# A two-layer SSD and HGRN2 trunk on one core: weight sums begun one iteration later, a spill cut into four, two gate operations given priority, and new amounts of filling work

## The chip, the cores and the metric

The kernel runs on one core of a Trainium2 chip. The core has a matrix engine (TensorE, PE in the profile), a vector engine (VectorE, DVE), a scalar engine that evaluates functions and copies (ScalarE, ACT), a general engine (GpSimd, POOL), and SyncE (SP), which here only issues transfers. Each engine takes its own instructions one after the other in a fixed order, and instructions on different engines wait for each other through semaphores. Transfers between the chip's memory (HBM) and the core's memory (SBUF) run in queues; the two that matter here are the one that SP issues (q1 in the profile) and the one that POOL issues (q0). The results of matmuls stand in PSUM, in banks of 128x512 numbers of 4 bytes.

The metric is the device time of one execution in microseconds (us), as the median of several executions. Less is better.

## The reference, cut to what matters

Two layers work on x of 512 tokens by 1024 features. Layer 0 mixes tokens with a Mamba-2 SSD (inner width 2048, 32 heads of 64, 4 groups, state 128), layer 1 with HGRN2 (8 heads of 128).

```python
for i in range(2):
    mix = ssd_mixer(x, ...) if i == 0 else hgrn2_mixer(x, ...)
    h = layer_norm(ALPHA * x + mix)
    h = layer_norm(ALPHA * h + square(relu(h @ w1)) @ w2)        # w1: 1024 x 4096
    x = h + sigmoid(h @ ple_w_gate[i]) * (p[i] @ ple_w_proj[i])  # p[i]: 512 x 256
# ssd_mixer:   z, xbc, dt = split(u @ w_in); xbc = silu(conv4(xbc)); scan over chunks of 128;
#              y = rms_norm((scan + d * xs) * silu(z)); y @ w_out
# hgrn2_mixer: q, fz, v, g = split(u @ w_in); k = (1 - lb) * sigmoid(-fz); scan over chunks;
#              rms_norm(o) * silu(g) @ w_out
```

All of it is in 32-bit floating point.

## The kernel before, in words

**Products.** The kernel gives TensorE operands of the type `fp32r`; it writes every operand as a high part and a low part and forms each product with three matmuls (`mm3`, lines 120 to 122: high by high, high by low, low by high). For weights, `unit` (line 103) loads 512 KB into a `raw` buffer through SP's queue; ACT casts it to `whi` (line 114), DVE subtracts for `wlo` (line 116), and PE takes them as they are done. The pools have 3 `raw` buffers, 6 of `whi` and 6 of `wlo`, 9 of a larger kind called `b8`, and 4 PSUM banks called `pj`. A unit is 1.05 us of ACT, 1.22 us of DVE and, in the SSD stage, 24 matmuls.

**Who sets the order.** The order of PE's instructions is the order of the code, by hand (`tc.manual_schedule`). Those of ACT, DVE, POOL and SP are put into an order at build time by a scheduler, which goes by readiness in its own model and by priorities: `high_priority(LEAD)` for weights (100), `high_priority(TURN)` for some steps of the gate (200); `behind(x)` keeps an instruction from being issued ahead of x. On the chip the order is then fixed: an instruction that waits holds all that stand behind it on its engine.

**SSD stage (0 to some 340 us).** After a start that makes the token operand out of four chunks of x and runs the first group of products (`py`, lines 170 to 174), a loop over k = 1 to 8 holds one product of 128 channels after the other: `x_part(2k)`, `x_part(2k+1)` (products whose convolution starts with ACT's line 810 and ends with line 816), `z_part(2k-2)`, `z_part(2k-1)` (silu in line 866, `sz`), `decays` (exponentials on ACT, lines 900 to 914, L907, L911 and L912 among them), `states`, `mixed`, and `finish` (which normalises; ACT's line 976 makes `ri`). The z parts stand so for k = 2 to 6; `z_part(12)` follows at k = 7, and `z_part(13)`, `z_part(14)` and, later, `z_part(15)` at k = 8. DVE's line 246 adds a piece of the output product from a `pj` bank into `acc`.

**Sums of weights.** HGRN's v and g products, and the MLPs', use a block product of 2 x 2 blocks with seven products in place of eight; its operands are sums of blocks of the weights and of the tokens. The sums of the weights for HGRN are made during the SSD stage, by `sums_early` (line 426): eight pieces, each a `b8` buffer, four loads of 256 KB on POOL's queue (line 433), two steps of two DVE operations (lines 436 to 441), and two steps of two ACT casts (line 448), two DVE subtractions (line 449) and four stores to `pre_h` (lines 450 and 451). So a piece is five steps, and all of them 40; the loop calls `next(sums)` at five places per k, from k = 1 on.

**Gate of layer 0 and start of HGRN (to some 790 us).** `mlp_and_gate` ends with the gate h @ gate, whose `finish(c, h, sg)` (line 662) multiplies a product by `sg` (line 669) and adds it to `acc` (line 670). Afterwards `turn` (line 620) transposes a chunk of `acc` on PE (line 624) into the operand of HGRN; ACT and DVE split it (lines 627 and 628), and `mix_part` (line 593) makes the sums of tokens. The last two turns stay in the list `late`.

**HGRN.** The scan's instructions on PE leave it idle unless other products stand between them. `background` (line 1198) is a generator of such products, one matmul triple at a time: the first eight triples of `gated(0)`, the late turns, a spill of all of `acc` (2 MB, line 1204, POOL's queue) to `xd`, since `blocks_late` (line 1147, copies in lines 1153 and 1154) takes the memory of `acc`, and then the entries of `JOBS`: `q0` to `q7` are `qf` (a head's q and f products; ACT copies the first into `qx`, line 1167, and makes f and k of the second, lines 1171 and 1174), `s` is `blocks_late`, `b0` and `b1` are `gated(0)` and `gated(1)` (the v and g products; each holds two `pj` banks, and line 1142 adds its last ones to v), `o` the first half of the output product. `restore` reads `xd` back. `fill(n)` takes n us of that work; `GAPS` has an n for each gap between the scan's stages, a row for each pair of heads. The first matmul on a tile v is in line 1409.

Of the kernel before, what the change touches and what calls it, by code (L numbers as in the profile page):

```python
# [29 lines left out]
TURN = 200  # L30
# [3 lines left out]

JOBS = "q0 q1 s q2 q3 b0 q4 q5 q6 q7 b1 o".split()
LEADIN = 6.0
GAPS = (6.0, 12.0, 9.0, 9.0), (11.0, 10.0, 10.0, 10.0), (10.5, 10.5, 10.5, 10.5), (10.5, 7.0, 4.0, 3.5), (3.0, 2.0, 2.5, 0.0)
CONSTS = dict(ident=P, triu=P, eps=1, convw=96, convb=24, dskip=16, snw=16, dtc=2, hlb=8, hnw=1)
# [3 lines left out]
def trunk(ctx: ExitStack, tc, a):  # L42
# [382 lines left out]
    def sums_early(w, dst):  # L425

        for u in range(2):
            for h in range(2):
                cs = slice(h * 512, (h + 1) * 512)
                t = mk(b8, [P, 4, T], "b8", F32R)  # L430
                w00, w01, w10, w11 = (f32(t)[:, i] for i in range(4))
                for x, src in zip((w00, w01, w10, w11), (w[0][0], w[0][1], w[1][0], w[1][1])):
# [82 lines left out]
    def mlp_and_gate(layer, h_s, last, turns=()):  # L515
# [79 lines left out]
        def mix_part(h, c, v):  # L595

            cs = slice(c % 2 * P, c % 2 * P + P)
            if not mix:
                mix["keep"] = mk(b8, [P, 2, 4, 256], "b8")
            k0, k1 = (mix["keep"][:, i, :, cs] for i in range(2))  # L600
            if c < 2:
                if h:
                    nc.vector.tensor_sub(k0, v, k0)
                else:
                    nc.scalar.copy(k0, v)
                return
            if c == 2:
                mix["s2" if h else "s3"] = mk(b8, [P, 2, 4, 256], "b8", F32R)
            if h:
                nc.vector.tensor_add(k1, v, k1)  # L610
                nc.vector.tensor_sub(k0, k1, k0)
                put("s2", cs, k0)
            else:
                nc.scalar.copy(k1, v)
                s3 = tmp("sg", [P, T]).rearrange("p (j t) -> p j t", j=4)
                nc.vector.tensor_sub(s3, k0, v)
                put("s3", cs, s3)
# [42 lines left out]
        def finish(c, h, sg):  # L660
# [5 lines left out]
            for i, part in enumerate(pp):  # L666
                cs = slice(i * n, (i + 1) * n)
                d = acc[:, c, h * 512 + i * n : h * 512 + (i + 1) * n]
                nc.vector.tensor_mul(sg[:, cs], part, sg[:, cs])
                (nc.vector if i == len(pp) - 1 else nc.gpsimd).tensor_add(d, sg[:, cs], d)  # L670
                if last:
# [324 lines left out]
    heads = [[[[whvg[8 * i + 4 * n + 2 * r + u] for u in range(2)] for n in range(2)] for r in range(2)] for i in range(2)]  # L996
    sums = (step for i in range(2) for step in sums_early(heads[i], a["pre_h"][i]))

    PIECES = {3: (0, 4), 4: (2, 2), 5: (0, 4), 6: (2, 2)}

    with tc.manual_schedule(engines={mybir.EngineType.PE}):
# [8 lines left out]
        for k in range(1, 9):  # L1010
# [11 lines left out]
            states(k - 1)  # L1022
            next(sums)
            decays(i - 1)
            some(mine)
            next(sums)
            if k < 8:
                load_decay(i)
                x_part(j)
                load_decay(j)  # L1030
            if k in (3, 5, 7):
                outs = pieces(k // 2 - 1, rms_group(k // 2 - 1, bank(psy, "py0")))
            some(theirs)
            next(sums)
            if k == 1:
# [10 lines left out]
            if k == 2:  # L1046
                nc.sync.dma_start(acc, a["x"])
                for c in range(NCH):
                    nc.vector.tensor_scalar(acc[:, c, :], acc[:, c, :], ALPHA, None, ALU.mult)
            next(sums)  # L1050
            done = [mixed(i - 2), (mixed(i - 1))] if k != 7 else [mixed(12)]
# [7 lines left out]
            for t, d in enumerate(done):  # L1059
                finish(i - 2 + t, *d)  # L1060
            next(sums)
        some(3)
# [135 lines left out]
    def background():  # L1198
# [3 lines left out]
        for f in late:  # L1202
            f()
        nc.gpsimd.dma_start(a["xd"], acc)
        for job in JOBS:
            i = int(job[1:] or 0)
            if job == "o":
                yield from out0()
            elif job == "s":
                blocks_late()  # L1210
            elif job[0] == "q":
# [389 lines left out]
```

## Time and profile before

| | us |
|---|---|
| median of 3 runs (1401.05 to 1402.51) | 1402.27 |
| the profiled execution, whole | 1401.34 |
| its span (first to last instruction) | 1399.6 |
| TensorE busy in it | 1387.8 (99%) |
| VectorE busy | 1104.3 (79%) |
| ScalarE busy | 820.5 (59%) |
| GpSimd busy | 62.6 (4%) |

The mean granted clock of TensorE is 0.999. Times inside the kernel are counted from the start of the span. A row of the timeline has the start, the duration, the engine, the line, the operation, its output and inputs (buffer numbers left out), and, in brackets, how long the engine stood idle ahead of it and what ended that. A row of the waits has the waiting engine's operation, what it waited for, the sum in us, how many times, and the largest. Matmuls are pipelined: each takes some 0.4 us, and the next one starts before it ends.

### The profile page before, as it was taken

How to read it: one execution, taken by the hardware profiler on the slowest of the kernel's cores; microseconds unless marked ns; L12 is line 12 of the kernel's file. 1: busy time of each engine (PE TensorE's matmuls, PEld its weight loads, DVE VectorE, ACT ScalarE, POOL GpSimd, SP SyncE). 2: the span in 40 equal slices, each digit the busy share in tenths (PEclk: the TensorE clock that was granted, in tenths of full speed). 3: DMA queues.
4: the chain of work that ended last, by engine and by line, in shares of the span. 5: the costliest groups of instructions: out<-in, count | busy, mean ns of one | idle time of the engine just before them, and what ended most of it. 6: DMA issues, size and time to landing. Idle time of an engine off the chain costs nothing.

```text
span 1399.6 us, 20799 instructions
## 1 busy us (share of the span) xinstructions
PE 1387.8 (99%) x7909; PEld 1159.1 (83%) x7909; DVE 1104.3 (79%) x1750; ACT 820.5 (59%) x1329; POOL 62.6 (4%) x122
## 2 busy tenths in 40 slices
PE   9999999999999999999999999999999999999998
PEld 7888888888888888888887788888898888888887
DVE  7898887788867879778888766768785887779886
ACT  6897777596455455546465355464455464555563
POOL 0121210211000000000000000000000000000000
PEclk9999999999999999999999999999999999999999
DMA  7566555554364665654384553464173656646364
GB/s 288 201 232 208 195 177 185 204 176 163 113 206 149 216 220 166 212 191 154 118 303 167 198 194 109 152 228 150 61 256 114 213 175 223 215 159 207 106 237 157
DMA packets 79252, 258.75 MB, mean 185 GB/s; under 512 B 9776, under 2 KB 10416, under 8 KB 78896
## 3 DMA queue, kind: packets, MB, share of 16 engines
q1 hardware_dynamic: 60096, 206.03, 43.9%
q0 software_dynamic: 9840, 34.61, 7.0%
q10 hardware_dynamic: 9216, 16.78, 3.3%
q8 instruction: 62, 1.02, 0.3%
q14 instruction: 38, 0.31, 0.1%
HBM read 219.57 MB, written 37.81 MB: 184 GB/s over the span
## 4 chain that ended last, share of the span: by engine, by line
PE 92%; ACT 3%; DVE 2%; DMA 1%; issue 1%; SPq 0%; DVEq 0%; ACTq 0%
PE pj L120 23%; PE pj L121 23%; PE pj L122 23%; PE py L120 5%; PE py L121 5%; PE py L122 5%; PE py L940 1%; DMA raw<-in_whq 1%; PE py L1256 1%; ACT b L907 1%; DMA a<-in_xw 1%; DVE wlo L116 1%; PE py L942 1%; PE pt L923 0%; ACT whi L114 0%
## 5 line engine op out<-in xcount | busy, mean ns | idle before, releaser
L120 PE MATMUL pj<-b,whi 128*128 128x512 f32 (+1 forms) x1000 | 380.0, 380 | 2.0 <-ACT qx L1167 1.6
L122 PE MATMUL pj<-b,wlo 128*128 128x512 f32 (+1 forms) x1000 | 377.4, 377 | 0.0
L121 PE MATMUL pj<-b,whi 128*128 128x512 f32 (+1 forms) x1000 | 377.2, 377 | 0.0
L116 DVE TENSOR_TENSOR wlo<-raw,whi 128x1024 fp32r<-128x1024 f32 x218 | 264.6, 1220 | 114.7 <-ACT whi L114 112.6
L114 ACT CAST whi<-raw 128x1024 fp32r<-128x1024 f32 x218 | 228.1, 1050 | 205.6 <-PE pj L121 79.1
L120 PEld LDWEIGHTS pj<-b,whi 128*128 128x128 f32 x1000 | 188.0, 188 | 37.4 <-ACT qx L1167 2.0
L122 PEld LDWEIGHTS pj<-b,wlo 128*128 128x128 f32 x1000 | 188.2, 188 | 34.7
L121 PEld LDWEIGHTS pj<-b,whi 128*128 128x128 f32 x1000 | 188.2, 188 | 34.0
L122 PE MATMUL pj<-whi,b 128*128 128x512 f32 (+1 forms) x482 | 187.4, 389 | 0.0
L120 PE MATMUL pj<-whi,b 128*128 128x512 f32 x448 | 176.7, 395 | 0.0
L121 PE MATMUL pj<-wlo,b 128*128 128x512 f32 x448 | 174.4, 390 | 0.0
L114 ACT CAST whi<-r 128x1024 fp32r<-128x1024 f32 x64 | 67.2, 1053 | 90.2 <-PE pj L121 67.9
L122 PEld LDWEIGHTS pj<-whi,b 128*128 128x128 f32 x482 | 90.5, 188 | 18.8 <-DVE b L1451 0.2
L120 PE MATMUL py<-whi,b 128*128 128x512 f32 x256 | 100.4, 392 | 0.0
L116 DVE TENSOR_TENSOR wlo<-r,whi 128x1024 fp32r<-128x1024 f32 x64 | 77.7, 1219 | 28.2 <-ACT whi L114 26.9
L122 PE MATMUL py<-whi,b 128*128 128x512 f32 x256 | 99.7, 389 | 0.0
L121 PE MATMUL py<-wlo,b 128*128 128x512 f32 x256 | 99.6, 389 | 0.0
L120 PEld LDWEIGHTS pj<-whi,b 128*128 128x128 f32 x448 | 84.1, 188 | 17.4 <-ACT b L1450 0.3
L121 PEld LDWEIGHTS pj<-wlo,b 128*128 128x128 f32 x448 | 84.2, 188 | 16.8
L120 PEld LDWEIGHTS py<-whi,b 128*128 128x128 f32 x256 | 48.1, 188 | 10.2 <-DVE acc L495 0.5
L122 PEld LDWEIGHTS py<-whi,b 128*128 128x128 f32 x256 | 48.0, 188 | 10.0
L121 PEld LDWEIGHTS py<-wlo,b 128*128 128x128 f32 x256 | 48.1, 188 | 9.7
(422 smaller groups left out, 2142.1 us busy)
## 6 DMA issues: line engine op xcount, KB each, us to landing
raw<-in_w SPq DMA_DIRECT2D x112, 512.0 KB, 3.8
r<-in_w SPq DMA_DIRECT2D x64, 512.0 KB, 4.1
raw<-in_wssd SPq DMA_DIRECT2D x38, 512.0 KB, 5.0
b<-in_whvg POOLq DMA_DIRECT2D x32, 256.0 KB, 6.8
a<-csd SPq DMA_DIRECT2D x16, 512.0 KB, 4.0
pre_h<-whi POOLq DMA_DIRECT2D x32, 256.0 KB, 2.5
pre_h<-b POOLq DMA_DIRECT2D x32, 256.0 KB, 3.2
raw<-in_wso SPq DMA_DIRECT2D x16, 512.0 KB, 4.3
```

The lines of the kernel that those rows point to most:

```text
L114: nc.scalar.copy(hi[:, :n], f)
L116: nc.vector.tensor_sub(lo[:, :n], f, f32(hi[:, :n]))
L120: nc.tensor.matmul(out, sh, mh, start=start, stop=False, **kw)
L121: nc.tensor.matmul(out, sh, ml, start=False, stop=False, **kw)
L122: marks["pe"] = nc.tensor.matmul(out, sl, mh, start=False, stop=stop, **kw)
L907: nc.scalar.activation(m[:, r, sl], csb[:, r, sl], AF.Relu, scale=-1.0, bias=cs_tok[:, c, 2 * j + r : 2 * j + r + 1])
L940: nc.tensor.matmul(yd[64 * r : 64 * r + 64, sl], xdt[:, c, r, :], m[:, r, sl], start=True, stop=c == 0)
L942: nc.tensor.matmul(yd[64 * r : 64 * r + 64, sl], pv[:, c - 1, r, :], ecs[:, r, (c - 1) * P : c * P], start=False, stop=True,)
L1256: nc.tensor.matmul(ps[r][32 * b : 32 * b + 32, base + n * c : base + n * c + n], kk[r][:, ts], moving(r, 4 * c + b), start=True, stop=True,)
```

## The change

1. `JOBS` has `q0 s0 q1 s1` where `q0 q1 s` stood, and the spill is cut into four transfers of 512 KB: chunks 2 and 3 of `acc` go in `mix_part` (second half of the features), chunk 0 at `s0`, and chunk 1 at `s1`, where `blocks_late` follows.
2. `GAPS` has other numbers.
3. In layer 0, the multiplication and the addition of `finish` in the second half of the features get the priority `TURN`.
4. The sums of weights begin at k = 2, with six steps per k in place of five. The four loads of a piece wait for a small POOL copy (128x4) out of `toks`, into the buffer that the loads fill.

```diff
-JOBS = "q0 q1 s q2 q3 b0 q4 q5 q6 q7 b1 o".split()
+JOBS = "q0 s0 q1 s1 q2 q3 b0 q4 q5 q6 q7 b1 o".split()
-GAPS = (6.0, 12.0, 9.0, 9.0), (11.0, 10.0, 10.0, 10.0), (10.5, 10.5, 10.5, 10.5), (10.5, 7.0, 4.0, 3.5), (3.0, 2.0, 2.5, 0.0)
+GAPS = (6.0, 12.0, 10.0, 10.0), (13.0, 9.5, 9.5, 9.5), (10.0, 10.0, 10.0, 10.0), (12.5, 6.0, 4.0, 3.5), (3.0, 2.0, 2.5, 0.0)
...
                 t = mk(b8, [P, 4, T], "b8", F32R)
+                nc.gpsimd.tensor_copy(f32(t)[:, :, 0], toks[0][:, :, 0])
...
                 put("s2", cs, k0)
+                nc.gpsimd.dma_start(a["xd"][:, c], acc[:, c])
...
-                nc.vector.tensor_mul(sg[:, cs], part, sg[:, cs])
-                (nc.vector if i == len(pp) - 1 else nc.gpsimd).tensor_add(d, sg[:, cs], d)
+                with tc.high_priority(offset=0 if last or not h else TURN):
+                    nc.vector.tensor_mul(sg[:, cs], part, sg[:, cs])
+                    (nc.vector if i == len(pp) - 1 else nc.gpsimd).tensor_add(d, sg[:, cs], d)
...
+    def step():
+        if k > 1:
+            next(sums, None)
...
             states(k - 1)
-            next(sums)
+            step()
             decays(i - 1)
             some(mine)
-            next(sums)
+            step()
             if k < 8:
                 load_decay(i)
                 x_part(j)
                 load_decay(j)
+            step()
...
             some(theirs)
-            next(sums)
+            step()
...
-            next(sums)
+            step()
             done = [mixed(i - 2), (mixed(i - 1))] if k != 7 else [mixed(12)]
...
             for t, d in enumerate(done):
                 finish(i - 2 + t, *d)
-            next(sums)
+            step()
...
-        nc.gpsimd.dma_start(a["xd"], acc)
         for job in JOBS:
...
-            elif job == "s":
-                blocks_late()
+            elif job[0] == "s":
+                nc.gpsimd.dma_start(a["xd"][:, i], acc[:, i])
+                if i:
+                    blocks_late()
```

Since sums, priorities and transfers stand elsewhere, the scheduler gives ACT, DVE, POOL and SP another order. Three places follow. Line numbers in the changed kernel are 1 to 9 higher: 449 for 448, 813 for 810, 869 for 866, 910 and 915 for 907 and 912, 672 and 673 for 669 and 670, 630 for 628, 1161 for 1153, 1175 for 1167. The numbers at the end of a name count buffers.

ACT's order in the SSD stage at k = 2, before. `whi_897` is the high half of the weights of z_part(2), and `cv_637` belongs to a product two ahead of x_part(4) and x_part(5) (the group of B and C at k = 1).

```order
L810 ACTIVATE cv_637<-pj_605,cst_160 128x512
L448 CAST whi_755<-b_83_540 128x512
L114 CAST whi_897<-raw_895 128x1024
L816 ACTIVATE xs_594<-cv_595 128x512
L900 ACT_TABLE_LOAD
L900 ACTIVATE cd_723<-a_561 128x8
L900 ACTIVATE cd_723<-a_601 128x8
```

ACT's order at the same place of the changed kernel: `cv_858` belongs to the convolution of x_part(5), and `whi_880` and `whi_913` are the weights of z_part(2) and z_part(3).

```order
L813 ACTIVATE cv_785<-pj_753,cst_160 128x512
L910 ACTIVATE b_808<-a_594,toks_455 128x128 x8
L914 ACTIVATE ecs_817<-a_594 128x768
L915 ACTIVATE b_808<-b_808 128x1024
L813 ACTIVATE cv_858<-pj_826,cst_160 128x512
L449 CAST whi_868<-b_130_802 128x512
L114 CAST whi_880<-raw_878 128x1024
L114 CAST whi_913<-raw_911 128x1024
```

The cast for z_part(2) stood right behind the first convolution of that group, and so ahead of x_part(4) and x_part(5); now it stands behind the first step of the convolution of x_part(5) and behind one cast of a sum (line 449).

ACT's order at k = 8, before. `whi_3042` is the high half of the weights of z_part(15), and `sz_2812` belongs to z_part(12).

```order
L976 ACT_TABLE_LOAD
L976 ACTIVATE ri_2775<-ri_2775,cst_160 128x4
L114 CAST whi_3042<-raw_3040 128x1024
L866 ACT_TABLE_LOAD
L866 ACTIVATE sz_2812<-pj_2781 128x512
L816 ACTIVATE xs_2761<-cv_2762 128x512
L114 CAST whi_3116<-raw_3114 128x1024
```

ACT's order at k = 8 of the changed kernel. `sz_3016` belongs to z_part(14), and `whi_3068` is the high half of the weights of z_part(15).

```order
L869 ACT_TABLE_LOAD
L869 ACTIVATE sz_3016<-pj_2985 128x512
L915 ACT_TABLE_LOAD
L915 ACTIVATE b_3031<-b_3031 128x1024
L449 CAST whi_3047<-b_486_2922 128x512 x2
L449 CAST whi_3056<-b_486_2922 128x512
L114 CAST whi_3068<-raw_3066 128x1024
```

The cast for z_part(15) stood ahead of the silu of z_part(12); now it stands behind that of z_part(14), a decay's exponential (line 915) and three casts of the last piece of the sums.

DVE's order at the end of the gate, before. `sg_6627` is the last product of the gate, and the rows of lines 628 and 603 (`pt`) belong to a turn.

```order
L116 TENSOR_TENSOR wlo_6764<-raw_6760,whi_6762 128x1024
L593 TENSOR_TENSOR b_1092_6562<-b_1057_6324,b_1092_6562 128x4x128
L628 TENSOR_TENSOR b_1019_6133<-pt_6636,b_1017_6131 128x4x128
L603 TENSOR_TENSOR b_1057_6324<-pt_6636,b_1057_6324 128x4x128
L669 TENSOR_TENSOR sg_6627<-pj_6629,sg_6627 128x512
L116 TENSOR_TENSOR wlo_6801<-raw_6797,whi_6799 128x1024
L670 TENSOR_TENSOR acc_94<-sg_6627,acc_94 128x512
```

DVE's order at the same place of the changed kernel, where `sg_6637` is that last product; `pm_6611` belongs to the turn ahead of the one just shown, whose rows (of `pt`) stand further down now.

```order
L116 TENSOR_TENSOR wlo_6740<-raw_6736,whi_6738 128x1024
L594 TENSOR_TENSOR b_1092_6570<-b_1057_6332,b_1092_6570 128x4x128
L672 TENSOR_TENSOR sg_6637<-pj_6639,sg_6637 128x512
L630 TENSOR_TENSOR b_1019_6141<-pm_6611,b_1017_6139 128x4x128
L673 TENSOR_TENSOR acc_94<-sg_6637,acc_94 128x512
L611 TENSOR_TENSOR b_1057_6332<-pm_6611,b_1057_6332 128x4x128
L116 TENSOR_TENSOR wlo_6773<-raw_6769,whi_6771 128x1024
```

The multiplication and the addition of the last product stood behind both turns; they now stand ahead of the last one, between the operations of the one before it, with one subtraction for a weight fewer between them.

ACT's order at the start of HGRN, before: `qx_6758` is the copy of the first q product, and line 1153 makes the two blocks that take the memory of `acc`.

```order
L114 CAST whi_6874<-raw_6872 128x1024
L627 CAST b_1017_6131<-pm_6718 128x4x128
L114 CAST whi_6917<-raw_6915 128x1024
L114 CAST whi_7024<-raw_7022 128x1024
L1167 COPY qx_6758<-pj_6733 128x32x16
L1153 CAST acc_6867<-b_1057_6324 128x1024 x2
L114 CAST whi_7117<-raw_7115 128x1024
```

ACT's order at the same place of the changed kernel.

```order
L629 CAST b_1017_6139<-pm_6728 128x4x128
L1161 CAST acc_6878<-b_1057_6332 128x1024
L114 CAST whi_6885<-raw_6883 128x1024
L1161 CAST acc_6878<-b_1057_6332 128x1024
L114 CAST whi_6928<-raw_6926 128x1024
L1175 COPY qx_6767<-pj_6742 128x32x16
L114 CAST whi_7035<-raw_7033 128x1024
L114 CAST whi_7128<-raw_7126 128x1024
```

The copies of line 1153 (now 1161) stood behind `qx`; they now stand ahead of it, and two of the three casts of weights that were ahead of `qx` have changed places with it.

More of the change, by code (lines that the diff above doesn't have):

```diff
@@ L996, in trunk @@
     heads = [[[[whvg[8 * i + 4 * n + 2 * r + u] for u in range(2)] for n in range(2)] for r in range(2)] for i in range(2)]
-    sums = (step for i in range(2) for step in sums_early(heads[i], a["pre_h"][i]))
+    sums = (n for i in range(2) for n in sums_early(heads[i], a["pre_h"][i]))
+    def step():
+        if k > 1:
+            next(sums, None)
     PIECES = {3: (0, 4), 4: (2, 2), 5: (0, 4), 6: (2, 2)}
```

## The prediction

> **What bounds the kernel.** I read the page first (the busy times), then TensorE's waits, then the places at which the change acts, engine by engine in the timeline, and the chain of waits. The page gives PE 99% of the span.
>
> ```profile
> PE 1387.8 (99%) x7909; PEld 1159.1 (83%) x7909; DVE 1104.3 (79%) x1750; ACT 820.5 (59%) x1329; POOL 62.6 (4%) x122
> ```
>
> So an edit gains only where PE stands still, and costs wherever it makes PE stand still. The whole list of PE's waits:
>
> ```profile
> PE py L120 <- ACT whi L174: 1.6, 2, 1.0
> PE pj L120 <- ACT qx L1167: 1.6, 1, 1.6
> PE pm L624 <- DVE acc L670: 1.5, 1, 1.5
> PE pt L1409 <- DVE a L1142: 1.4, 2, 0.9
> PE pm L155 <- DVE y L152: 1.1, 1, 1.1
> PE pj L120 <- DVE acc L246: 0.4, 1, 0.4
> ```
>
> That is 7.6 us, and five of the six entries lie where the diff acts. The list understates the start, where matmuls are merely spaced out. PE's timeline there:
>
> ```profile
> 6.53 0.40 PE L120 MATMUL py<-b,whi 128*128 128x512 f32 x1
> ...
> 8.64 0.51 PE L120 MATMUL py<-b,whi 128*128 128x512 f32 x1 [0.57 <-ACT whi L174]
> ...
> 11.62 0.50 PE L120 MATMUL py<-b,whi 128*128 128x512 f32 x1 [1.02 <-ACT whi L174]
> ...
> 16.54 0.39 PE L122 MATMUL py<-b,wlo 128*128 128x512 f32 x1
> ...
> 21.37 0.39 PE L122 MATMUL py<-b,wlo 128*128 128x512 f32 x1
> 21.59 0.39 PE L120 MATMUL pj<-b,whi 128*128 128x512 f32 x1
> ```
>
> Dense matmuls stand 0.22 to 0.23 us apart (21.37 to 21.59). From 6.53 to 16.54 there are 30 of them: 29 steps, 6.6 us dense, and they took 10.0.
>
> **The start.** The first piece of the weight sums no longer loads at the start. The DMA view of 4 to 10 us, and the total of 10.5 to 14.5 us:
>
> ```profile
> q0 software_dynamic: 295, 1.00, 49.2%
> q1 hardware_dynamic: 420, 0.99, 46.0%
> ```
>
> ```profile
> DMA packets 638, 1.61 MB, mean 403 GB/s; under 512 B 71, under 2 KB 166, under 8 KB 638
> ```
>
> q1 carries the chunks of x that those matmuls wait for; q0 carries the 1 MB of the sums. Alone, q1 ran at 403 KB/us, so its 0.99 MB would have taken 2.5 us in place of 6.0: 3.5 us sooner. PE's own dense work allows 10.0 - 6.6 = 3.4. I take **-3.4**; the ends are -1.6 (the listed waits alone) and -3.5.
>
> **k = 2.** Here the same shift of the sums puts things in PE's way. ACT's timeline, then PE's:
>
> ```profile
> 69.47 1.05 ACT L114 CAST whi<-raw 128x1024 fp32r<-128x1024 f32 x1 [1.26 <-DMA raw<-in_wssd]
> ...
> 88.81 0.76 ACT L810 ACTIVATE cv<-pj,cst 128x512 f32<-128x512 f32 x1
> 89.47 0.61 ACT L448 CAST whi<-b 128x512 fp32r<-128x512 f32 x1
> ```
>
> ```profile
> 85.12 0.39 PE L122 MATMUL pj<-b,wlo 128*128 128x512 f32 x1
> 85.35 0.39 PE L120 MATMUL pj<-b,whi 128*128 128x512 f32 x1
> ```
>
> The last matmul of x_part(5) ends at 85.51, and z_part(2) follows at once at 85.35, because both z units were cast by 70.5. In the changed order ACT casts z_part(2)'s unit only behind the convolution's first product of x_part(5) (`cv`, line 810), which needs that last matmul, and behind one cast of a sum. From 85.51: 0.66 (88.81 to 89.47) + 0.61 + 1.05 = 87.8 for the high half. DVE's wlo takes another 1.22 (row below): 89.0, where PE wants it with its third matmul, 0.45 after 85.35, at 85.8. That is a stall of **+3.2**; its floor is 2.4, the high half alone. It moves with PE, so the start cannot save it: 3.4 is won at 21 us and 3.2 is given back at 85.
>
> **k = 3.** From 70.5 to 115.7 ACT has hardly a gap, and then DVE runs into PE. The chain of waits, and ACT's row between:
>
> ```profile
> 114.61 1.05 ACT b L912
> ...
> 123.26 1.22 DVE wlo L116
> 125.06 0.76 DVE acc L246
> 125.86 0.50 PE pj L120
> ```
>
> ```profile
> 122.12 0.30 ACT L976 ACTIVATE ri<-ri,cst 128x4 f32<-128x4 f32 x1
> ```
>
> PE waits at z_part(4) for the bank that L246 drains, L246 for `ri`, and that for ACT's L976. Between the convolution of x_part(5) and L976 the changed ACT order has 10 table loads for 6, 9 casts of L114 for 6 and 8 of L448 for 6: 4 x 1.28 + 3 x 1.05 + 2 x 0.55 = 9.4 us more (1.28, 1.05 and a third of 1.64 are rows here and under k = 8). But ACT starts on that stretch when PE has done x_part(5), at 85.51 - 3.4 = 82.1 in place of 88.81, 6.7 sooner, since casts that lay ahead of it are gone. So L976 stands at 122.12 - 6.7 + 9.4 = 124.8 and is done at 125.1; the reciprocal and L246 (0.76) follow, and PE starts at about 126.2. The terms so far would put it at 125.7, so this is **+0.5**. Ends: -0.4 (the listed wait disappears too) and +3 (casts of sums held up by DVE's additions).
>
> **k = 8.** All four remaining steps of the last piece now stand ahead of z_part(15) or just behind it. ACT's and PE's rows of before:
>
> ```profile
> 298.60 1.06 ACT L114 CAST whi<-raw 128x1024 fp32r<-128x1024 f32 x1 [0.66 <-PE pj L121]
> ...
> 319.50 0.60 ACT L866 ACTIVATE sz<-pj 128x512 f32<-128x512 f32 x1
> 320.11 1.28 ACT L912 ACT_TABLE_LOAD   x1
> 321.41 1.06 ACT L912 ACTIVATE b<-b 128x1024 f32<-128x1024 f32 x1
> 322.37 1.64 ACT L448 CAST whi<-b 128x512 fp32r<-128x512 f32 x3
> ```
>
> ```profile
> 316.27 0.40 PE L122 MATMUL pj<-b,wlo 128*128 128x512 f32 x1
> ...
> 317.61 0.58 PE L120 MATMUL pj<-b,whi 128*128 128x512 f32 x1
> ```
>
> z_part(14) ends at 316.67 and z_part(15) starts at 317.61; its unit had been cast at 298.60. Now that cast comes behind `sz` of z_part(14), the table load, L912 and three casts of the sum: 0.61 + 1.30 + 0.96 + 1.64 + 1.06 = 5.57 after 316.67, so 322.2, and L116 (1.22) at 323.5, against the third matmul at 318.3: **+5.2**. ACT's backlog decides whether it is more. Before, it reached `sz` at 319.50, 2.8 late; three L114 (3.1) leave the stretch ahead, so the backlog about vanishes, and I take **+5.4**, with ends 4.6 (the high half alone) and 8.0 (all the backlog stays).
>
> The trace and the Trainium skill differ on that table load. Its page "ScalarE: Activation LUTs", section "What ACT_TABLE_LOAD costs", gives a switch 1.28 us for the load and about 1.38 more for a drain, 2.66 in all. In the rows above the load takes 1.28 and the activation starts 1.30 after it, so the trace shows the load and no drain. By the page k = 8 would be 1.4 dearer and the four more loads of k = 3 another 5.5: 1411.0 in place of the forecast.
>
> **The end of the gate and HGRN.** DVE around the last gate addition, ACT ahead of the first q product, and the spill (DMA view, 745 to 790):
>
> ```profile
> 759.79 0.68 DVE L669 TENSOR_TENSOR sg<-pj,sg 128x512 f32<-128x512 f32 x1
> ...
> 761.52 0.68 DVE L670 TENSOR_TENSOR acc<-sg,acc 128x512 f32<-128x512 f32 x1
> ```
>
> ```profile
> 773.86 1.04 ACT L114 CAST whi<-raw 128x1024 fp32r<-128x1024 f32 x1 [7.22 <-DMA raw<-in_whq]
> ...
> 775.29 2.00 ACT L1153 CAST acc<-b 128x1024 fp32r<-128x1024 f32 x2
> ```
>
> ```profile
> xd<-acc POOLq DMA_DIRECT2D x1, 2048.0 KB, 10.9
> ```
>
> With priority L669 and L670 come ahead of two operations of the turn and of one L116, over 2 us sooner than 761.5: PE's 1.5 us wait goes, **-1.5**. The 2 MB spill goes in four parts of 512 KB, two of them ahead of the last gate products, so the raw load that landed at 773.8 shares with a quarter of it. The `qx` copy also moves ahead of that row's cast, though behind both copies of blocks_late (1.0 each) and two casts (1.05 each). The copies wait for the last 512 KB, a quarter of 10.9 us after some 762: 765 + 4.1 = 769 for `qx`, and PE asked for it at 773.86 + 1.04 + 0.6 - 1.6 = 773.9. **-1.6**. Queued behind those copies are two casts that PE wants 10 us later.
>
> The gaps: the last product of gated(0) now ends 15 matmuls ahead of L1409 in place of 3, that of gated(1) 12 in place of 9; at 0.23 each the first wait (0.5) goes and 0.7 of the second (0.9): **-1.1**, ends -1.4 and -0.4. Other stages lose 3 to 6 matmuls of cover, 0.7 to 1.4 us; none of them waits in the trace. I take +0.3, ends 0 and +1.4.
>
> **At nothing:** POOL's copies ahead of the sums' loads (POOL is 4% busy), and the 3 MB that now load at once at about 43 us: they share with weights that are cast long before use (the row at 69.47 is for 90.8). On POOL's queue the stores stand behind those loads, and PE reads what they store only in the gate and HGRN. The loads ahead of PE could lag by a us or two, which the range holds.
>
> **Sum:** -3.4 + 3.2 + 0.5 + 5.4 - 1.5 - 1.6 - 1.1 + 0.3 = **+1.8**. The profiled execution took 1401.34 (span 1399.6), 0.9 under the median of 1402.27; it would become 1403.1, the median 1404.1. About 0.2%, 2.8 us, is what a measurement of this kernel can tell from no change, and this lies inside.
>
> **Rivals.**
> *ACT at k = 3 decides (slower).* If ACT reaches L976 later than worked out, every us is PE's. For: DVE is as full there as ACT, and casts of sums wait for its additions. Against: ACT enters sooner. With k = 3 at its end of +3 and, as casts of sums are then late in k = 8 too, 6.5 there: 1404.1 + 2.5 + 1.1 = 1407.7. It makes the whole slower by over 0.2% from 1 us of lateness on.
> *The unit casts do not hold PE (faster).* If ACT had both units in time after all, k = 2 and k = 8 would cost nothing: -3.4 - 0.4 - 1.5 - 1.6 - 1.1 = -8.0, 1394.3. For: in before no unit ever held PE in this stage. Against: an engine takes its rows in order, and both casts stand behind a row that needs PE's group just ahead.
> *ACT stands still around a switch of tables.* By the rows at 320.11 and 321.41 the whole of it is 0.02 us, so five more switches would give 0.1: 1404.2. The page named above says more; no row bears it out.
> That the moves are not made is no rival: the order shows every one of them.
>
> **Chances.** The forecast 0.50 (its own range 1401 to 1407), ACT at k = 3 0.30, casts in time 0.13, switches 0.02, a stall elsewhere that I did not find 0.05. The range leaves out the fast rival, the switches at the page's price and the tails: 1399.5 to 1408.5. Slower by over 0.2%: 0.30 + 0.02 + 0.05 = 0.37. Faster by over 0.2%: 0.13 and 0.02 from the forecast's tail, 0.15. Within: 0.48.
>
> **What would show it.** First pj matmul at about 18.2 in place of 21.6; a wait of PE on L114 or L116 of about 3 us near 82 to 85; one of about 5 near 318, on the same lines; none left on L670, `qx` or L174. Wrong, if no such wait stands at 318, or if z_part(4) starts before 124 or after 128.

## The result and the profile after

The changed kernel takes 1416.53 us (median of 4 runs, 1416.14 to 1418.07), the kernel before 1402.39 (4 runs, 1401.05 to 1402.53): a ratio of 1.0105, with a 95% interval of 1.0088 to 1.0123. It is slower by 14.1 us. The forecast was 1404.1, in a range of 1399.5 to 1408.5. The profiled execution took 1418.07 (span 1416.1), 16.7 more than that of before.

The busy times, and the whole list of TensorE's waits in the changed kernel (what waited, for what, the sum in us, how often, the longest):

```profile
PE 1395.3 (99%) x7909; PEld 1163.0 (82%) x7909; DVE 1106.4 (78%) x1750; ACT 831.1 (59%) x1336; POOL 67.6 (5%) x133
```

```profile
PE pj L120 <- ACT whi L114: 9.2, 2, 6.1
PE pt L926 <- DVE xdt L894: 3.9, 2, 3.7
PE pm L155 <- DVE y L152: 1.1, 1, 1.1
PE pj L122 <- DVE wlo L116: 1.0, 2, 0.5
PE pj L120 <- DVE acc L246: 0.9, 1, 0.9
PE py L976 <- DVE ss L971: 0.3, 1, 0.3
```

The waits on line 670, on `qx`, on the tiles of v and on line 174 are gone, as forecast. Two waits on a cast of weights have come, as forecast, and one on `xdt` that was not. All of them make 16.4 us where before had 7.6; that is 8.8 more, and the time grew by 16.7. So half of the loss is not in the list of waits. It shows in the granted clock: three stretches of the changed kernel, one behind each of the long waits (columns: length, TensorE's busy time, granted clock, DMA share, GB/s):

```profile
86.16:92.98 6.82, 6.28 (x16) 0.50 0.70 233
205.63:209.02 3.39, 3.39 (x9) 0.50 0.51 160
331.92:342.14 10.22, 6.33 (x14) 0.50 0.68 215
```

In before the clock is 1.00 until TensorE's last matmul. In these stretches a matmul takes 0.63 us in place of 0.39, and the next one starts 0.43 us later in place of 0.23. Where the loss arises is read from the same matmuls in both traces. From TensorE's timeline of before, those whose rows do not stand in the prediction (k = 5, the product behind z_part(15), and the second q product):

```profile
196.91 1.03 PE L923 MATMUL pt<-xw,btok 128*128 128x256 f32 x4
...
323.25 0.39 PE L120 MATMUL pj<-whi,b 128*128 128x512 f32 x1
...
775.44 0.50 PE L120 MATMUL pj<-b,whi 128*128 128x512 f32 x1 [1.57 <-ACT qx L1167]
```

And from that of the changed kernel the first pj product, z_part(2) and its third matmul, z_part(4), k = 5, z_part(15) and what follows it, and the second q product:

```profile
18.73 0.39 PE L120 MATMUL pj<-b,whi 128*128 128x512 f32 x1
...
85.75 0.50 PE L120 MATMUL pj<-b,whi 128*128 128x512 f32 x1 [3.10 <-ACT whi L114]
...
87.18 0.80 PE L122 MATMUL pj<-b,wlo 128*128 128x512 f32 x1 [0.54 <-DVE wlo L116]
...
130.58 0.50 PE L120 MATMUL pj<-b,whi 128*128 128x512 f32 x1 [0.94 <-DVE acc L246]
...
205.44 1.87 PE L926 MATMUL pt<-xw,btok 128*128 128x256 f32 x4 [3.67 <-DVE xdt L894]
...
335.33 0.79 PE L120 MATMUL pj<-b,whi 128*128 128x512 f32 x1 [6.12 <-ACT whi L114]
...
344.54 0.39 PE L120 MATMUL pj<-whi,b 128*128 128x512 f32 x1
...
793.65 0.39 PE L120 MATMUL pj<-b,whi 128*128 128x512 f32 x1
```

| TensorE reaches | before | after | later by | lost since the row above |
|---|---|---|---|---|
| the first pj product | 21.59 | 18.73 | -2.86 | -2.9 (start) |
| z_part(2) | 85.35 | 85.75 | 0.40 | 3.3 (wait 3.1) |
| z_part(4) | 125.86 | 130.58 | 4.72 | 4.3 (waits 0.5 and 0.5 more than before; clock 3.3) |
| the states of k = 5 | 196.91 | 205.44 | 8.53 | 3.8 (wait 3.7) |
| z_part(15) | 317.61 | 335.33 | 17.72 | 9.2 (wait 6.1; clock of k = 5 1.7; the rest small, 0.5 of it listed waits at k = 7) |
| the product behind it | 323.25 | 344.54 | 21.29 | 3.6 (wait 0.5; clock 3.1) |
| the second q product | 775.44 | 793.65 | 18.21 | -3.1 (L670, `qx`) |
| the end of the span | 1399.6 | 1416.1 | 16.5 | -1.7 (tiles of v and the rest) |

### The profile page after: what moved, and what is told of

It reads as the page before. It is cut to its first block, busy times and chain, and to the rows that moved or that the text cites. A ratio compares the mean times of both kernels' runs of the same rounds, so it can differ in the third digit from the quotient of the medians.

```text
span 1416.1 us, 20834 instructions
## 1 busy us (share of the span) xinstructions
PE 1395.3 (99%) x7909; PEld 1163.0 (82%) x7909; DVE 1106.4 (78%) x1750; ACT 831.1 (59%) x1336; POOL 67.6 (5%) x133
## 4 chain that ended last, share of the span: by engine, by line
PE 79%; issue 8%; DVE 4%; ACT 3%; DMA 3%; POOL 2%; SPq 0%; POOLq 0%; DVEq 0%; ACTq 0%
PE pj L120 20%; PE pj L122 20%; PE pj L121 19%; PE py L120 5%; PE py L122 5%; PE py L121 5%; DMA b<-in_whvg 2%; DVE wlo L116 1%; POOL b L434 1%; PE py L1265 1%; ACT b L910 1%; POOL pre_h L451 1%; POOL pre_h L452 1%; DVE cv L816 1%; DMA raw<-in_wssd 0%
## 5 line engine op out<-in xcount | busy, mean ns | idle before, releaser
L120 PEld LDWEIGHTS py<-whi,b 128*128 128x128 f32 x256 | 48.1, 188 | 10.1 <-DVE acc L496 0.5
L122 PEld LDWEIGHTS py<-whi,b 128*128 128x128 f32 x256 | 48.1, 188 | 10.1
```

The costliest lines, as they stand in the source:

```text
L120: nc.tensor.matmul(out, sh, mh, start=start, stop=False, **kw)
L122: marks["pe"] = nc.tensor.matmul(out, sl, mh, start=False, stop=stop, **kw)
```

## Experiments

Medians of timed runs against before on the same chip; a ratio stands with its 95% interval. The median of before lies between 1401.5 and 1402.4 us in the groups of runs below and in the result, so a difference between two runs of different groups holds to about 0.9 us.

### Which part costs: e1 and e2

e1 is the changed kernel with the sums of before; e2 is before with the change's fourth part alone. The edit of e1:

```diff
-                nc.gpsimd.tensor_copy(f32(t)[:, :, 0], toks[0][:, :, 0])
...
-        if k > 1:
-            next(sums, None)
+        next(sums, None)
...
-            step()          # the sixth, behind load_decay(j)
```

> Parts 1 to 3 alone (spill in four, gaps, priority), with the sums of weights as before. Theory A (all of the loss comes from the shifted sums; the other parts gain what TensorE's four waits at the end of the gate and in HGRN gave up between the two traces, 4.4 us): 1398.0. Rival B (the new spill, gaps and priority carry part of the loss): 1402.4 or more.

> Part 4 alone (sums from k = 2, six steps per k, loads behind the small copy). Theory A: the changed kernel's time without the 4.4 us that the other parts gain, 1420.9; TensorE waits of some 3, 4 and 6 us at k = 2, 5 and 8, each followed by a granted clock of 0.5. Rival B: 1416 or less.

e1 took 1396.80 us, ratio 0.9967 (0.9954 to 0.9980); e2 1421.22, ratio 1.0143 (1.0126 to 1.0160). The other parts gain 4.7 and the sums cost 19.8; the two sum up to 15.1, against 14.1 for the whole change. Theory A was 1.2 us off in e1 and 0.3 in e2. TensorE's whole list of waits in e1:

```profile
PE py L120 <- ACT whi L174: 1.4, 2, 0.8
PE pm L155 <- DVE y L152: 1.1, 1, 1.1
PE pj L120 <- DVE acc L246: 0.5, 1, 0.5
```

The three waits of the gate and of HGRN are gone, and the start is as it was. In e2 they are all there, beside the three of the SSD stage (9.2 on line 114, 2.8 on `xdt`).

### Is it the waiting that halves the clock: e3, e9 and e13

e3 gives TensorE work where it waited:

```diff
         ps = bank(psj, "pj")
+        for _ in range({z_part(2): 14, z_part(15): 27}):
+            nc.tensor.matmul(ps, x_s.h(0, slice(0, P)), x_s.h(0), start=True, stop=True)
```

> The changed kernel with extra matmuls, whose result the product then overwrites: 14 ahead of z_part(2) and 27 ahead of z_part(15), 3.2 and 6.1 us of work that nothing needs, where TensorE waited 3.1 and 6.1 us. Theory C (the clock falls to a half because TensorE stood idle, and costs 3.0 us at k = 2 and 3.1 at k = 8 on top of the waits): the clock stays at 1.00 at both places and the time falls by 6.1 to 1410.4. Rival D (the half clock has another cause, or the casts are what is late in any case and the clock costs nothing): 1416.5, or up to 9 more if the added matmuls delay the path.

e3 took 1414.21 us, ratio 1.0089 (1.0074 to 1.0104). The clock at the same two places:

```profile
86.16:92.98 6.82, 6.14 (x27) 1.00 0.67 214
331.92:342.14 10.22, 9.25 (x41) 1.00 0.84 281
```

So work that nothing needs brought the full clock back: theory C. The time fell by 2.3 (by 1.4 when each kernel is set against before in its own group) and not by 6.1. TensorE, earlier now, stood longer elsewhere: its waits on `xdt` at k = 5 and k = 7 together sum up to 4.7 in place of 3.9, those on line 116 to 1.6 in place of 1.0, that on line 246 is 1.3 in place of 0.9.

e9 puts waits of known kind into the MLP, e13 into the SSD stage, both on the kernel of e8 (below), whose list of TensorE's waits adds up to 2 us:

```diff
+        nc.tensor.matmul(ps[0:32, 0:32], pad, pad, start=True, stop=True)
+        for _ in range(n):
+            nc.gpsimd.memset(pad, 0.0)
+        nc.tensor.matmul(ps[0:32, 0:32], pad, pad, start=True, stop=True)
         project(w, x_s, ps)
```

> The kernel of e8 with six waits of TensorE of known kind in the MLP of layer 0, where it otherwise stands nowhere: a tiny matmul, 4, 10, 16, 22, 30 and 44 small fills on GpSimd that come behind it, and a tiny matmul that waits for the last of them; at 0.14 us a fill and some 0.2 for the signals that is about 0.8, 1.6, 2.4, 3.3, 4.4 and 6.4 us, 19 in all. Theory C (a wait of up to some 2 us costs its length, one of 3 us or more brings one to three stretches of 3.4 us at half clock, worth 1.5 to 3 us): a clock of 0.5 behind the three longest and none behind the two shortest; 1393.4 + 19 + 5 to 9 = 1417 to 1421. Rival D (the half clock does not come from standing still): clock 1.00 all through, 1412.

> The kernel of e8 with six known waits in the SSD stage, where TensorE's order is written by hand and nothing can be drawn ahead of them: ahead of x_part(4), (6), (8), (10), (12) and (14) a tiny matmul, 8, 14, 18, 22, 28 and 40 small fills on GpSimd of 0.12 us each, and a tiny matmul that waits for the last. With 0.25 for the signals that is 1.2, 2.0, 2.5, 3.0, 3.7 and 5.2 us, 17.6 in all. Theory C: no half clock behind the first, one or two stretches of 3.4 us of it behind each of the last three, the second and third open; 1393.4 + 17.6 + 5 to 9 = 1416 to 1420. Rival D (the half clock of the changed kernel does not come from standing still): 1411, clock 1.00 all through.

e9 took 1405.50, ratio 1.0022 (1.0012 to 1.0031), and told little: the order in the MLP is the scheduler's, which drew other matmuls into the waits. The longest that was left was 2.0 us, and one stretch of half clock followed it; the others were 1.3 and less, and none followed.

e13 took 1431.81, ratio 1.0216 (1.0201 to 1.0232). Its six waits were longer than planned; then the clock behind each (the first two stretches are at 1.00):

```profile
72.17 0.25 PE L828 MATMUL pj<-pad 128*32 128x32 f32 x2 [1.52 <-POOL pad L827]
...
104.04 0.25 PE L828 MATMUL pj<-pad 128*32 128x32 f32 x2 [2.68 <-POOL pad L827]
...
157.70 0.32 PE L828 MATMUL pj<-pad 128*32 128x32 f32 x2 [3.41 <-POOL pad L827]
...
204.76 0.27 PE L828 MATMUL pj<-pad 128*32 128x32 f32 x2 [4.14 <-POOL pad L827]
...
261.83 0.32 PE L828 MATMUL pj<-pad 128*32 128x32 f32 x2 [5.24 <-POOL pad L827]
...
311.36 0.32 PE L828 MATMUL pj<-pad 128*32 128x32 f32 x2 [7.43 <-POOL pad L827]
```

```profile
72.40:79.00 6.60, 6.60 (x30) 1.00 0.63 194
104.30:111.00 6.70, 6.70 (x31) 1.00 0.27 95
157.07:163.89 6.82, 6.19 (x16) 0.50 0.27 95
204.85:208.26 3.41, 3.41 (x10) 0.50 0.28 103
259.47:266.28 6.81, 4.45 (x12) 0.50 0.32 111
307.25:317.48 10.23, 6.12 (x16) 0.50 0.53 199
```

A wait of 1.5 or 2.7 us cost its own length; each of the four longer ones brought one, two or three stretches of 3.41 us at half clock. The busy time in them sums up to 20.2 us, half of which is lost: 10.1. With the waits (24.4) and the 12 pairs of tiny matmuls (some 3, at 0.25 to 0.32 a pair) that makes some 37 of the 38.4 us that e13 is above e8. Rival D falls, and the term is sized: waits of 3.4 to 7.4 us cost 1.7 to 3.1 more than they last. The Trainium skill, "TensorE: Matmul & The Clock Gate", section "What's actually happening", says the same: windows of some 3.4 us, half the clock after an idle one, the full clock after a busy one. The runs agree, but for the limit: waits of 2.0 us (e9) and 2.8 (e2), shorter than a window, have already brought a stretch.

How a wait lies decides between such cases, and the traces above show it. Within one trace the stretches begin whole multiples of 3.413 us apart: in e13 those at 157.07, 204.85, 259.47 and 307.25 lie 14, 16 and 14 of them apart, in the changed kernel those at 86.16, 205.63 and 331.92 lie 35 and 37. So a trace can be cut into windows of that length, and TensorE's idle time counted in each. The wait of 2.0 us in e9 lay inside one window, and the next had half clock. That of 2.7 us in e13 lay across an edge, and no half clock followed (two windows of e9, then two of e13; idle time is the length less the busy time):

```profile
621.68:625.09 3.41, 1.40 (x8) 1.00 0.22 43
625.10:628.51 3.41, 3.41 (x9) 0.50 0.95 303
...
99.04:102.45 3.41, 2.32 (x21) 1.00 1.03 404
102.46:105.86 3.40, 1.82 (x9) 1.00 0.90 340
```

Counted so in all sixteen traces of this case, every window at full clock with 2.0 us or more of idle time was followed by half clock, and none with 1.9 or less, but for one at the start of e11 (1.6). Half clock went on for another window where TensorE had stood for more than some 0.5 us in the one before. The windows lie otherwise in each trace: the same wait of 3.1 us at z_part(2) brought two stretches in the changed kernel and one in e6. So part of the price of a wait of 2 to 4 us is luck.

### What holds the units at k = 2 and k = 8: e5, e7 and e12

In the parts of ACT's order that stand with the change, the numbers of the `whi` buffers rise from row to row, that is, the casts that first use a buffer come in the order in which the code asks for one; the casts of the sums draw on the same pool. With six steps per k, a cast of a sum stands ahead of z_part(2) and two ahead of z_part(15) in the code; with five, from k = 1 on, they stood behind. That is theory F. e5 holds the steps of k = 8 back until z_part(15) has been asked for; e12 does so and moves the fourth step of k = 2 behind z_part(3); e7 leaves the places and gives the sums' casts a buffer of their own:

```diff
 # e5 and e12: no step at k = 8 ahead of
                 z_part(15)
 # e12: at k = 2
-            step()
                 z_part(i - 2)
                 z_part(i - 1)
+                step()
 # e7
-    whip = pool("whip", 6)
+    whip = pool("whip", 5)
+    sump = pool("sump", 1)
```

> The changed kernel with the steps of k = 8 put behind z_part(15) in the code (what is then left over runs at the loop's end). Theory F (a sum's cast takes its buffer from the weights' own six, and first uses of these buffers come in the order of the code, so the casts that stand ahead of z_part(15) in the code hold its unit): the wait at z_part(15) and the half clock behind it go, 6.1 + 0.5 + 3.1 = 9.7 us: 1406.8. Rival G (ACT is so far behind at k = 8 that the unit is late wherever the sums stand): a wait of 3 us or more stays there, 1411 or more.

> The changed kernel with one buffer of its own for the casts of the sums, and five in place of six for the casts of the weights. Theory F: the units of z_part(2) and z_part(15) no longer queue behind a sum's cast; both waits and their half clock go (6.6 at k = 2, 9.7 at k = 8), k = 5 stays: 1400.2. Rival G: waits of 2 us or more stay at k = 2 and k = 8, 1410 or more. A third way: five buffers are too few for the weights elsewhere, which shows as new waits on lines 114 and 116 outside these places.

> The changed kernel with its six steps per k, but the casts of k = 2 put behind z_part(3) in the code, and the steps of k = 8 behind z_part(15). Theory F (places in the code alone hold the units): no wait on lines 114 and 116 in the SSD stage, 6.6 + 9.7 us less; the wait at k = 5 stays: 1400.2. Rival N (ScalarE and VectorE are as late at k = 3, so that what is won at k = 2 is lost at the bank that line 246 drains): a wait of 2 to 3 us there, with half clock, 1403 to 1406.

e5 took 1410.96 (1406.84 to 1412.95), ratio 1.0061 (1.0039 to 1.0082): the wait at z_part(15) and its half clock are gone, while the steps left over make a wait of 2.6 us behind the loop (on line 971). e12 took 1408.38, ratio 1.0043 (1.0027 to 1.0059): no wait on line 114 or 116 is left, but rival N holds too, and the time is above its range, since a wait of 2.7 us behind the loop (line 971) brings another stretch of half clock. Its z_part(4), and the clock from there:

```profile
126.47 0.79 PE L120 MATMUL pj<-b,whi 128*128 128x512 f32 x1 [3.15 <-DVE acc L246]
```

```profile
125.70:132.40 6.70, 5.93 (x14) 0.50 0.71 238
```

What holds z_part(4) in e12 is VectorE's row. ScalarE has `ri` ready at 123.08, but VectorE makes the reciprocal of it only at 124.99, behind subtractions for a sum and for a weight:

```profile
122.78 0.30 ACT L979 ACTIVATE ri<-ri,cst 128x4 f32<-128x4 f32 x1 [0.51 <-DVE ri L978]
...
123.86 1.23 DVE L116 TENSOR_TENSOR wlo<-raw,whi 128x1024 fp32r<-128x1024 f32 x1
124.99 0.18 DVE L980 RECIPROCAL ri<-ri 128x4 f32<-128x4 f32 x1
```

e7 took 1421.73, ratio 1.0133 (1.0117 to 1.0149), slower than the changed kernel. Its trace is of the fastest of its four runs (1417.31, mean clock 0.999; the others took 1421.21 to 1422.33 at 0.996), so some 4 us of half clock, an estimate from these clocks, are not in it. Its units came in time (0.3 us on the cast in the whole kernel), so the mechanism is as theory F says, yet the time is not: line 246 (247 in its count) makes TensorE wait 2.8 us at k = 3, with half clock, and five buffers make new waits in the MLPs and at the gate.

```profile
PE pj L122 <- DVE wlo L117: 2.9, 2, 1.4
PE pj L121 <- DVE acc L247: 2.8, 1, 2.8
...
PE pj L121 <- ACT whi L115: 0.3, 1, 0.3
```

### What holds TensorE at k = 5: e6 and e14

VectorE stands at the first addition of a piece until its load has landed, and behind that addition stand `finish` and the turn's operations, up to the `xdt` that TensorE needs. The load was issued late: GpSimd's row has the eight stores of the piece ahead in front of it, which wait for casts, which wait for that piece's own additions. The rows of the changed kernel, VectorE's and GpSimd's (the first store of the fourth piece, and the loads of the fifth):

```profile
195.22 0.69 DVE L437 TENSOR_TENSOR b<-b 128x512 f32<-128x512 f32 x1 [3.92 <-DMA b<-in_whvg]
```

```profile
178.59 0.54 POOL L451 DMA_DIRECT2D pre_h<-whi  x1 [9.09 <-ACT whi L449]
...
186.82 2.21 POOL L434 DMA_DIRECT2D b<-in_whvg  x4 [0.41 <-POOL b L431]
```

Both expectations below take this addition for the fourth piece's; VectorE's order shows that it is the fifth's. e6 leaves out the fourth piece's additions, e14 the third piece's stores, so that the fourth's loads, and all that follows them, come sooner:

```diff
 # e6, fourth piece only
-                    nc.vector.tensor_sub(w11, w11, w01)
-                    nc.vector.tensor_sub(w01, w01, w00)
...
-                    nc.vector.tensor_add(w00, w11, w00)
-                    nc.vector.tensor_sub(w10, w10, w00)
 # e14, third piece only
-                            nc.gpsimd.dma_start(dst[n, u, 0][:, cs], f32(hi))
-                            nc.gpsimd.dma_start(dst[n, u, 1][:, cs], f32(x))
```

> The changed kernel without the four additions and subtractions on VectorE of the fourth piece of the sums (part of the weights of HGRN is then not summed). Theory H (at k = 5 VectorE stands 3.9 us at the first of these, for a load that came late, and TensorE waits for what stands behind it): the wait of 3.7 us on line 894 and its 1.4 us of half clock go, 1411.4. Rival I (VectorE waits in its row for ScalarE's casts of y, line 964, and is late without the sums as well): a wait of 2 us or more stays at k = 5, 1414 or more.

> The changed kernel without the eight stores of the third piece of the sums (that part of pre_h is filled with stores of the last piece instead, so its values are others), so that the fourth piece's loads no longer stand behind them on GpSimd's queue; the order of VectorE and ScalarE there is the same. Theory H (at k = 5 it is the late load alone that holds VectorE and so TensorE): no idle time of VectorE ahead of line 437 there, the wait of 3.7 us on line 894 goes and its 1.4 of half clock: 1411.4. Rival O (the additions' own 2.8 us and the rest of VectorE's row hold it): a wait of 2 us or more stays, 1414 or more.

e6 took 1413.57, ratio 1.0083 (1.0068 to 1.0098). It settles little, since the additions that VectorE stands at were still there: they came 2.4 us sooner (192.80), after a wait of 4.5 us for the load, and TensorE's wait fell from 3.7 to 1.4. e14 took 1412.30, ratio 1.0077 (1.0061 to 1.0094), 4.2 less than the changed kernel (3.4 with each against before in its own group); TensorE's wait on `xdt` and its half clock are gone. VectorE's row at the same place in e14:

```profile
191.04 0.69 DVE L437 TENSOR_TENSOR b<-b 128x512 f32<-128x512 f32 x1 [3.67 <-DMA b<-in_whvg]
```

VectorE still stands there, against what theory H expected, but goes on 4.2 us sooner, and that is enough. The order on VectorE is the same in both, so it is the time at which the load lands that decides.

### The start's gain without the later sums: e4, e10 and e8; the gaps: e11

e4 adds to e1 a small copy that makes the first piece's loads wait for the token operand, e8 puts these four loads on SP's queue, e10 is the changed kernel with five steps per k, and e11 is e1 with the gaps of before:

```diff
 # e4
+                    nc.gpsimd.tensor_copy(f32(t)[:, :, 0], f32(x_s.l(7))[:, 0:4])   # first piece
 # e8
-                    nc.gpsimd.dma_start(x, src[u][:, cs])
+                    (nc.sync if first_piece else nc.gpsimd).dma_start(x, src[u][:, cs])
 # e10
-            step()          # the sixth; the last piece runs behind the loop
```

> Parts 1 to 3, the sums at five steps per k from k = 1 as before, and a small copy that lets the first piece's loads go only when the token operand is made. Theory A (the start's gain comes only from the loads that no longer share with the chunks of x, and needs no later sums): 1398.0 less 2.6, 1395.4, with no wait of over 2 us in the SSD stage. Rival E (the later loads push the first additions and casts into TensorE's way as the six steps did): 1398 or more, with a wait at k = 2 or 3.

> The changed kernel with five steps of the sums per k in place of six, from k = 2; the last piece runs behind the loop. Theory K (not the later start of the sums but their six steps per k do the harm: they put casts ahead of z_part(2) and z_part(15) in the code, and bring VectorE to a piece before its load is there): all three waits go and the start's gain stays: 1396.8 (parts 1 to 3) - 2.6 = 1394.2. Rival L (later sums are in the way wherever they stand): a wait of 2 us or more in the SSD stage, 1398 or more.

> Parts 1 to 3, the sums from k = 1 as before, with the loads of the first piece alone on SP's queue, behind the chunks of x, in place of POOL's. Theory A (the start is slow because the first piece's 1 MB shares with the chunks of x): the spacing goes at the start, 2.6 us less than parts 1 to 3 alone (1396.8): 1394.2. Rival J (the loads now stand ahead of the units of weights in SP's queue, or VectorE stands at the first addition as in the gated start): 1396.8 or more, with a wait of TensorE before 50 us.

> Parts 1 and 3 alone: the kernel of e1 with the gaps of before. Theory A with the gaps' own share (the two waits on the tiles of v, line 1142 of before, sum up to 1.4 us, and are there again): 1396.8 + 1.1 to 1.4 = 1398.1. Rival M (the spill and the priority alone make all of it, or the new gaps cost elsewhere what they gain there): 1396.8 or less.

e4 took 1400.01, ratio 0.9987 (0.9978 to 0.9996): rival E. VectorE stood 4.8 us at the first addition, ahead of the products' subtractions, TensorE waited 2.2 and 0.7 us, and the clock was halved for 3.4:

```profile
27.85 0.69 DVE L438 TENSOR_TENSOR b<-b 128x512 f32<-128x512 f32 x1 [4.81 <-DMA b<-in_whvg]
```

e10 took 1400.84, ratio 0.9992 (0.9982 to 1.0001). The three waits of the SSD stage are gone, as theory K says, but the time is that of rival L: the last piece behind the loop takes the gain back. ScalarE's cast of y comes 3.0 us late there, and the clock is halved for 6.8.

```profile
347.57 0.50 PE L120 MATMUL pj<-whi,b 128*128 128x512 f32 x1 [3.00 <-ACT b L964]
```

e8 took 1393.37 us, ratio 0.9937 (0.9922 to 0.9952). This is faster than before by 8.7 and than the changed kernel by 23. On SP's queue the loads come behind the chunks of x and yet early enough for the additions. TensorE is busy for 1385.8 of its 1391.8 us, and this is the whole list of its waits:

```profile
PE pm L155 <- DVE y L152: 1.1, 1, 1.1
PE py L120 <- ACT whi L174: 0.7, 1, 0.7
PE pj L121 <- DVE b L629: 0.2, 1, 0.2
```

e11 took 1398.57, ratio 0.9974 (0.9964 to 0.9983), 1.8 more than e1 (1.2 with each against before in its own group), and the wait of 1.4 us on the tiles of v is back. So the gaps give about what theory A expected of them (1.1 to 1.4), and rival M falls.

## Why the prediction was wrong

**The start** (-3.4) was right in kind: the matmuls are dense from 9.1 us on, and -2.9 came.

**k = 2** (+3.2) was right in its chain. The waits were 3.1 and 0.5, since ACT was still busy with line 915 when the product ended. The step that failed is the price: "That is a stall of +3.2". It cost 6.9, because 3.3 us of half clock came with it: the sum prices a wait by its length alone.

**k = 3** (+0.5) looks right at 0.5, but by luck. L976 was put at 124.8; it stood at 128.78 (line 979), 4 us later, and TensorE waited little only because it was itself 4 us later; z_part(4) started at 130.58, outside the 124 to 128 that the prediction named. Part of ScalarE's lateness came from TensorE's: ScalarE stood 2.1 us for its products (0.65, 0.47 and 0.93). With the half clock of k = 2 filled, in e3, line 979 (982 in its count) still stood at 126.45, 1.6 later than worked out, and z_part(4) waited 1.3. With the wait of k = 2 gone, in e12, whose ScalarE order is another, ScalarE was early (122.78) and z_part(4) waited 3.1 for VectorE. So there was a stall at k = 3 behind that of k = 2, as the rival had it, but in e12 VectorE makes it and not ScalarE.

**k = 8** (+5.4, ends 4.6 and 8.0) came as 6.1 + 0.5. ACT started `sz` 1.9 us after the product's end (329.81 against 327.92): a square for `finish` held it for 0.6, and the table load of `sz` itself, which the sum leaves out, for 1.3. The result lay between the ends. Its half clock of 3.1 us was not in them. No activation stood still behind the table load of line 915 there (load at 330.43, activation at 331.72), so the drain of 1.38 us that the Trainium skill gives ("ScalarE: Activation LUTs", section "What ACT_TABLE_LOAD costs") had no part in it.

**At nothing** stood the sums' loads: "The loads ahead of PE could lag by a us or two, which the range holds". What lagged was not a load ahead of PE but one ahead of VectorE, and by 4 us: the fifth piece's, with TensorE's operands behind it in VectorE's row. k = 5 cost 3.7 us of waiting and 1.7 of clock; "a stall elsewhere that I did not find" had a chance of 0.05. In e10, with five steps per k, this wait is not there.

**The end of the gate and HGRN** (-1.5 - 1.6 - 1.1 + 0.3 = -3.9) was right: -4.7 by e1, of which the gaps have 1.2 to 1.8 by e11. Two slips did no harm: its terms for the gaps, 0.5 and 0.7, make -1.2 and not -1.1, and by the orders shown with the change one cast of weights has changed places with `qx`, not two; the wait on `qx` is gone all the same.

In the profiled executions the miss is 15.0 us (1418.07 against 1403.1). Of it 8.1 are half clock (3.3, 1.7 and 3.1); 3.8 the wait at k = 5; 1.6 the longer waits at k = 2 and k = 8; 1.4 small losses between k = 5 and k = 8; 0.5 the start; some 0.5 is spread over the rest; and some 0.9 were gained at the gate and in HGRN beyond the forecast. With the clock in the sum, the two waits that were foreseen would alone have made some 1410.5 (1404.1 + 3.3 + 3.1), outside the range and slower beyond doubt. The profile of before could not show that price: its clock was 1.00 in every stage, and no wait in it was longer than 1.6 us. The Trainium skill, "TensorE: Matmul & The Clock Gate", section "HAM oscillation — how this bites in real kernels", does state it, a clock that falls to half behind a long wait and half of the throttled time lost, and it was not weighed against the two stalls.

**Open:** where between 1.9 and 2.0 us of idle time in a window the limit lies, and why the start of e11 fell below it. The windows were read from the traces; no run moved one wait along them.

## What to carry to other kernels

A wait of the matrix engine is priced by its length only while it is short. Here waits below 2 us in a dense stage cost their length; from 2 to 4 us the place of the wait decided, and from 4 us on there was always half clock. Add half of the busy time in each stretch that may come, 1.7 to 3.3 us here, and give the engine something to do where a long wait cannot be helped. Filler that shares a pool of buffers, an engine's row or a queue with the work on the path must stand behind that work in the code, not only have less priority. And a load that is in the way may only need another queue: behind what it disturbed, it cost nothing here.

## What the runs showed of the hardware

Half clock came in stretches of 3.41 us or two or three times that, on windows of 3.413 us whose place is fixed within an execution. The first stretch followed a window in which TensorE had stood for 2.0 us or more (2.01 in e9), so it began within the wait or up to 1.4 us behind it (e6), 1.8 at the start of e11; the last one was a window in which TensorE stood for some 0.5 us at most. Kernels with waits near that length scatter more: e5's four runs lie 6.1 us apart (mean clocks 0.995 to 0.998), those of e1, without long waits, 1.6 (0.999 to 1.000). The profiled execution of the changed kernel has a mean clock of 0.992, two of its other runs 0.994.
